# Eighteen column pairs of a SwiGLU gate/up stage as Strassen-Winograd block products, with an earlier LayerNorm sum moved between engines

## The chip, the cores and the metric

The kernel runs on one NeuronCore of a Trainium2 chip. The metric is the device time of one execution in microseconds (us), as a median over several executions. Five engines work side by side and wait for each other through semaphores: TensorE (PE in the profile; its weight loads are PEld), VectorE (DVE), ScalarE (ACT), GpSimd (POOL) and SyncE (SP, which here only issues DMAs). The program fixes the order of instructions on each of PE, DVE, ACT and POOL; an instruction that must wait holds up everything behind it on its own engine.

## The reference, cut to what matters

One layer of a hybrid decoder trunk: a modulated input projection, a convolution branch, dilated attention, a gated merge, a residual with LayerNorm (LN1), a modulated SwiGLU feed-forward network (FFN) and a second residual with LayerNorm. The change touches LN1 and the FFN:

```python
x = layer_norm(DN_ALPHA * x + (1 + g1) * y, ln1_g, ln1_b)
u = x * (1 + sc2) + sh2
h = (jax.nn.silu(u @ w_gate) * (u @ w_up)) @ w_down
x = layer_norm(DN_ALPHA * x + (1 + g2) * h, ln2_g, ln2_b)
```

There are 544 tokens (512 of a prompt, 32 of samples), `D_MODEL` is 1024 and `D_FF` is 2816, so 22 blocks of 128 columns. Everything is float32 in and out.

## The kernel before, in words

Activations lie transposed, channels on the 128 partitions and tokens on the free axis, and the tokens are cut into two halves h of 272. A float32 product is made from two fp32r parts of each operand: a high part, which ACT makes by a cast, and a low part, source minus high part, which DVE makes by a subtraction. A block of a matmul is then three matmuls: high weights by high data, high weights by low data, low weights by high data. `mm_group` (line 191) does this for a weight tile of eight 128x128 blocks along the inner dimension k: 8 x 3 matmuls of 272 columns for each half, 48 for both halves, each with its own weight load.

Weight tiles come through one stream in a fixed order: `load_more` (109) issues the DMA of a tile on SP as soon as one of four raw buffers is free, `prep_to` (119) splits a tile (ACT cast, line 131, then DVE subtraction, line 132) into one of three high and three low buffers, and `w_next` (138) hands out a tile and prepares up to three tiles ahead. Tiles of a kind other than None have places of their own, and are prepared only once a flag says that the place exists.

The output projection stage (loop at line 970) runs eight output blocks m for h = 0, then eight for h = 1. Each result is added to `z` (L983, and L987 and L989 for the samples). The class `Stats` (860) collects the LayerNorm sums on the way: at m = 3 a provisional mean by a matmul with ones (L887), by which `z` is shifted (L875), then sums `lns` of `z` (L878) and `lnq` of its squares (ACT L870, POOL L879). For h = 0 the engine of both sums is POOL; for h = 1 `lns` is on DVE. `finish` (904) ends the sums, adds over the partitions by matmuls with ones (L919, L920), and subtracts the mean (POOL L931, DVE L929). `ln1_gen` (935) then makes for each k the normalised value (DVE L946), the modulated input `u2` (ACT L948, for the samples POOL L950 and L951), its high part (ACT L952) and its low part (DVE L942), and for h = 1 turns `z` into the residual's input on POOL (L956). The generator is advanced between the blocks of the next stage.

The FFN (loop at line 1042) runs in three chunks of 8, 7 and 7 column blocks f. For each f the gate tile and the up tile are multiplied with `u2` of both halves, 96 matmuls, and `gu_evict` (1003) makes silu(gate) x up from the four PSUM tiles: sigmoid on ACT (L1008), two products on DVE (L1010, L1012), then the high part H on ACT (L1014) and the low part on DVE (L1016). After the f of a chunk, eight blocks m of the down projection over that chunk are added to `z` (`down_evict`, 1018). The first two f of the first chunk are split: the four tiles are first multiplied with half 0 alone (`first`, four PSUM tiles of the pool `pmm`), while LN1 of half 1 ends; then k by k with half 1 (`second`, lines 1061 to 1067, four PSUM tiles of other pools). The last chunk's down projection runs half by half, with the second LayerNorm's sums. Its weights are kept in places of their own (`wd0`, `wd1`), the first four prepared from the flag at line 1084 on.

`copies` (183) spreads DMA copies of the caches over the run; ACT issues them.

## Time and profile before

| | |
|---|---|
| median of 3 runs | 1046.74 us (1046.41 to 1048.29) |
| the profiled execution's own time | 1048.44 us |
| its span, first to last instruction | 1046.4 us |
| granted TensorE clock, mean | 0.990 |
| matmul instructions | 9168 |
| HBM read and written | 231.36 MB and 97.58 MB |

In the groups of instructions a line gives the source line, the engine, the operation, the tiles written and read, the shape of output and input and the count; then the busy time in us, the mean duration of one in ns, and the idle time of the engine just before, with what ended it. In the timeline a line gives the start and the duration in us; instructions of one line in a row are merged (x2), and the brackets hold the idle time before and what ended it. In the windows a line gives the stretch, its length, then for PE, PEld, DVE, ACT and POOL the busy time and count, the granted clock, the DMA share and GB/s. A matmul's duration contains its time in the pipeline; the distance from one start to the next is what it costs in a row of them. Durations of neighbouring DVE and POOL instructions overlap a little too, so there as well the distance of starts is the cost of one.

### The profile page before, as it was taken

Reading aid. Unit: us, or ns where it says so; the run is one execution under the profiler, and the core shown is the slowest. Engines: PE = TensorE matmul, PEld = TensorE weight load, DVE = VectorE, ACT = ScalarE, POOL = GpSimd, SP = SyncE. Lnnn points to the kernel's source line nnn. Section 1 sums busy time; section 2 is a strip of 40 time slices with the busy share of each in tenths; the row PEclk is TensorE's granted clock in tenths of the full one; section 3 lists DMA queues with packets and bytes.
Section 4 is the critical chain, followed back from the end, with each engine's and each line's share of the span. In section 5 each row is a group of like instructions: output and inputs, shape, how many; then the busy total and the mean of one; then the engine's idle time right before and its main releaser. Section 6 shows DMA issues by size and latency. Waiting matters only on the chain.

```text
span 1046.4 us, 21532 instructions
## 1 busy us (share of the span) xinstructions
PE 1006.8 (96%) x9168; PEld 964.8 (92%) x9168; DVE 564.4 (54%) x988; ACT 416.1 (40%) x798; POOL 153.4 (15%) x226
## 2 busy tenths in 40 slices
PE   4999999999999999999999989999999999999995
PEld 3887899999988989999999989999999999999994
DVE  3422688879886563342229767544333344344487
ACT  3312235545457666543433446422122231132333
POOL 0201010010014400101103747000000000000046
PEclk8999999999999999999999999999999999999998
DMA  9898687786785664799933710547854767754402
GB/s 379 328 387 323 248 299 257 257 330 238 279 304 187 214 258 152 293 362 391 374 123 122 246 42 21 200 163 259 287 196 167 251 231 266 252 188 172 127 15 86
DMA packets 44943, 242.64 MB, mean 232 GB/s; under 512 B 7408, under 2 KB 10736, under 8 KB 37680
## 3 DMA queue, kind: packets, MB, share of 16 engines
q1 hardware_dynamic: 34592, 126.83, 33.9%
q10 hardware_dynamic: 7632, 88.43, 23.2%
q0 software_dynamic: 2624, 26.02, 6.2%
q8 instruction: 72, 1.18, 0.4%
q14 instruction: 23, 0.19, 0.0%
HBM read 231.36 MB, written 97.58 MB: 314 GB/s over the span
## 4 chain that ended last, share of the span: by engine, by line
PE 78%; DVE 10%; ACT 5%; POOL 3%; issue 2%; DMA 2%; ACTq 0%; DVEq 0%; POOLq 0%
PE mm L196 23%; PE mm L197 22%; PE mm L199 22%; PE od L737 2%; PE Sd L702 2%; PE adaps L331 1%; DVE mrg L826 1%; DMA wr<-in_w_in 1%; PE pt L513 1%; DVE wl L132 1%; DMA cst<-in_cst 1%; PE o L529 1%; DVE z L1031 1%; DVE lns L878 1%; DVE P L498 1%
## 5 line engine op out<-in xcount | busy, mean ns | idle before, releaser
L196 PE MATMUL mm<-u,wh 128*128 128x272 f32 x1528 | 419.7, 292 | 0.0
L197 PE MATMUL mm<-u,wh 128*128 128x272 f32 x1528 | 412.5, 288 | 0.0
L199 PE MATMUL mm<-u,wl 128*128 128x272 f32 x1528 | 317.8, 288 | 0.0
L196 PEld LDWEIGHTS mm<-u,wh 128*128 128x128 f32 x1528 | 288.0, 188 | 14.2 <-issue 11.0
L197 PEld LDWEIGHTS mm<-u,wh 128*128 128x128 f32 x1528 | 287.9, 188 | 0.2
L199 PEld LDWEIGHTS mm<-u,wl 128*128 128x128 f32 x1528 | 239.7, 188 | 0.0
L132 DVE TENSOR_TENSOR wl<-wr,wh 128x1024 fp32r<-128x1024 f32 (+2 forms) x132 | 155.2, 1177 | 154.9 <-ACT wh L131 154.1
L131 ACT CAST wh<-wr 128x1024 fp32r<-128x1024 f32 (+2 forms) x132 | 130.5, 991 | 161.4 <-PE mm L197 135.7
L436 DVE SCALAR_TENSOR_TENSOR convy<-glu,vec,convy 128x512 f32<-128x512 f32 x120 | 95.6, 796 | 2.5
L197 PE MATMUL mm<-h,wh 128*128 128x272 f32 x240 | 64.8, 288 | 0.0
L196 PE MATMUL mm<-h,wh 128*128 128x272 f32 x240 | 64.5, 287 | 0.0
L1014 ACT CAST h<-sgf 128x272 fp32r<-128x272 f32 x44 | 17.0, 420 | 103.2 <-DVE sgf L1012 103.2
L896 POOL TENSOR_TENSOR lnq<-lnq,lnsq 128x272 f32<-128x272 f32 x4 | 3.1, 778 | 365.6 <-ACT lnsq L870 365.6
L1012 DVE TENSOR_TENSOR sgf<-sgf,mm 128x272 f32<-128x272 f32 x44 | 17.4, 434 | 63.3 <-PE mm L199 63.0
L1021 DVE SCALAR_TENSOR_TENSOR z<-mm,modT,z 128x272 f32<-128x272 f32 (+1 forms) x48 | 21.7, 479 | 55.5 <-PE mm L199 55.5
L199 PE MATMUL mm<-h,wl 128*128 128x272 f32 x240 | 49.6, 288 | 0.0
L634 ACT ACTIVATE qk<-mm,vec 128x272 f32<-128x272 f32 (+1 forms) x48 | 25.9, 626 | 56.6 <-PE mm L199 56.6
L196 PEld LDWEIGHTS mm<-h,wh 128*128 128x128 f32 x240 | 45.2, 188 | 0.0
L197 PEld LDWEIGHTS mm<-h,wh 128*128 128x128 f32 x240 | 45.2, 188 | 0.0
L506 ACT ACTIVATE P<-P,st 128x256 f32<-128x256 f32 x64 | 31.2, 489 | 28.2 <-DVE st L500 25.7
L197 PE MATMUL mm<-mrg,wo 128*128 128x272 f32 x128 | 37.8, 296 | 1.7 <-DVE mrg L826 1.7
L196 PE MATMUL mm<-mrg,wo 128*128 128x272 f32 x128 | 38.3, 299 | 0.0
(270 smaller groups left out, 1625.9 us busy)
## 6 DMA issues: line engine op xcount, KB each, us to landing
out_s<-in_c ACTq DMA_DIRECT2D x32, 2044.0 KB, 9.0
wr<-in_w_in SPq DMA_DIRECT2D x60, 512.0 KB, 6.9
wr<-in_w_gu SPq DMA_DIRECT2D x44, 512.0 KB, 4.8
KT<-in_kt SPq DMA_DIRECT2D x24, 792.0 KB, 7.0
VV<-in_vv SPq DMA_DIRECT2D x24, 768.0 KB, 7.5
gb<-in_w_ada POOLq DMA_DIRECT2D x8, 2048.0 KB, 16.7
...
```

Source lines behind the costliest of these rows:

```text
L131: act.copy(out=hv, in_=raw)
L132: dve.tensor_tensor(out=lv, in0=raw, in1=hv.bitcast(F32), op=ALU.subtract)
L196: pe.matmul(ps[h][:, :HC], lhsT=hi[:, k], rhs=A[h][:, 0, k], start=(k == 0), stop=False)
L197: pe.matmul(ps[h][:, :HC], lhsT=hi[:, k], rhs=A[h][:, 1, k], start=False, stop=False)
L199: pe.matmul(ps[h][:, :HC], lhsT=lo[:, k], rhs=A[h][:, 0, k], start=False, stop=(k == nk - 1))
L436: dve.scalar_tensor_tensor(out=o, in0=src, scalar=sc, in1=o, op0=ALU.mult, op1=ALU.add)
L506: act.activation(out=p[:, a:b], in_=p[:, a:b], func=AF.Exp, bias=st[:, kd, s, hh, 0:1], accum_out=st[:, kd, s, hh, 1:2])
L634: act.activation(out=o, in_=src, func=AF.Identity, bias=V("b_in", col))
L702: pe.matmul(S[32 * c:32 * c + 32, 132 * g:132 * g + 132], lhsT=q[:, col:col + 32], rhs=KT[:, j, c], start=(t == 0), stop=(j == 0 or t == 3))
L737: pe.matmul(o[32 * c:32 * c + 32, :], lhsT=lhsT, rhs=rhs, start=(j == 0), stop=(j == 9))
L1012: dve.tensor_tensor(out=sg[h], in0=sg[h], in1=pu[h][:, :HC], op=ALU.mult)
L1021: dve.scalar_tensor_tensor(out=zz[:, :n1], in0=ps[:, :n1], scalar=modT[:, 5, m, 0:1], in1=zz[:, :n1], op0=ALU.mult, op1=ALU.add)
```

## The change

For f = 3 to 20 the gate and up product of one f is taken as a product of 2x2 blocks. Rows are gate and up, columns are the token halves, the inner dimension is cut into k = 0..3 and 4..7. A11, A12 are the two k halves of the gate tile, A21, A22 those of the up tile; B11, B21 are the k halves of `u2` of half 0, B12, B22 those of half 1. Seven products of such blocks, 12 matmuls each, stand for eight:

- on the weight side POOL makes for each f S1 = A21 + A22, S2 = S1 - A11, S3 = A11 - A21, S4 = A12 - S2, each 128x512, in a ring `SS` of three buffers;
- on the data side four sums are made once: T1 = B12 - B11 (for S1), T2 = B22 - T1 (for S2), T3 = B22 - B12 (for S3), T4 = B21 - T2 (for A22). For this a tile `tf` takes B11 and B21 in one piece again (two POOL additions of 128x1088 of high and low part, issued after m = 3 of h = 1 of the output projection), and `ln1_gen` writes `u2a` of half 1 into it;
- the seven weight blocks, called units, are split one by one (ACT cast, DVE subtraction of 128x512), five units ahead of their use (`LEAD`), and the sums of f + 1 and its first five units are made during the products of f;
- `seven` adds the products in four PSUM tiles X, Zd, Y, Zc: A11 and A12 into X, S1 and S4 into Zd, S2 into Y, S3 and A22 into Zc, and builds the four results between the products, as each is due: X is gate of half 0, U2 = (first state of X) + Y, up of half 1 is U2 + Zc + Zd before their second products, up of half 0 is U2 + Zc after it, gate of half 1 is U2 + Zd after it. The last three steps (`rest`: p3, e1, e2) run during the first three products of the next f.

Blocks f = 0, 1, 2 and 21 stay as they were. In the down stages of the first two chunks the first units of the next f are made after m = 5, 6 and 7. H lies in the same two big tiles in all chunks. The flag of `wd0` is now set after f = 21. In LN1, `lns` of h = 0 goes from POOL to DVE, and L956 becomes eight POOL instructions `idle_work` during f = 3 and 4. One small scratch tile (`csg`) shares a buffer now.

```diff
--- before.py
+++ after.py
...
@@ -154,7 +156,8 @@
...
-            add_w(I["w_gu"][i], 8, ("gu", "gu", i - 3) if 3 <= i < 7 else None)
+            gu_at[i] = len(stream)
+            add_w(I["w_gu"][i], 8, ("gu", f"gu{i - 3}", 0) if 3 <= i < 5 else ("winograd",) if 6 <= i < 42 else None)
...
     def ln1_gen(h, stats):
         sd = yield from stats.finish(False, (0, 2) if h else ())
...
         for k in range(8):
...
             dve.tensor_tensor(out=zk, in0=zk, in1=sd, op=ALU.mult)
-            ak = a[k] = tmp4.tile([128, 512], F32, tag="P", name="u2a")[:, :HC]
+            ak = a[k] = tmp4.tile([128, 512], F32, tag="P", name="u2a")[:, :HC] if h == 0 else TF[0][:, 2 + k // 4, k % 4]
             act.activation(out=ak[:, :n1], in_=zk[:, :n1], func=AF.Identity, scale=G9[:, k, 0:1], bias=B9[:, k, 0:1])
             if h == 1:
...
-            if h == 1:
-                pool.tensor_scalar(out=zk, in0=zk, scalar1=agb[:, 0, k:k + 1], scalar2=agb[:, 1, k:k + 1], op0=ALU.mult, op1=ALU.add)
...
     wo = []
     for h in range(2):
-        stats = Stats(h, dve if h else pool)
+        stats = Stats(h, dve)
...
             if h == 1 and m == 3:
-                res["gu"] = [big_tile(i, [128, 4, 8, 128], F32R, f"gu{i}") for i in (0, 1)]
-                flags.add("gu")
+                TF.append(big_tile(0, [128, 4, 4, HC], F32, "tf"))
+                for i in range(2):
+                    pool.tensor_tensor(out=TF[0][:, i], in0=f32(u2[0][:, 0, 4 * i:4 * i + 4]),
+                                       in1=f32(u2[0][:, 1, 4 * i:4 * i + 4]), op=ALU.add)
...
+    UNITS = ("A11", "S1", "S2", "S3", "A12", "A22", "S4")
+    LEAD = 5
...
+    def add_up(f, n):
+        g, u = raw_of(f)
+        o = sums[f, n] = own["SS"][:, len(sums) % 3]
+        x, y, op = {
+            "S1": lambda: (u[:, 0:4], u[:, 4:8], ALU.add),
+            "S2": lambda: (sums[f, "S1"], g[:, 0:4], ALU.subtract),
+            "S3": lambda: (g[:, 0:4], u[:, 0:4], ALU.subtract),
+            "S4": lambda: (g[:, 4:8], sums[f, "S2"], ALU.subtract),
+        }[n]()
+        pool.tensor_tensor(out=o, in0=x, in1=y, op=op)
...
+    def unit_low():
+        if los:
+            f, j = los.pop(0)
+            hi, lo = place[f, j]
+            dve.tensor_tensor(out=lo, in0=src_of(f, UNITS[j]), in1=f32(hi), op=ALU.subtract)
+            if UNITS[j] == "A22":
+                assert (f, "S4") in sums
+                i = gu_at[2 * f]
+                done[i] = done[i + 1] = True
+                load_more()
+                assert pos["prep"] == i
+                pos["prep"] = i + 2
+
+    def unit_high(f, j):
...
+        else:
+            if j // 2 not in ring:
+                ring[j // 2] = (whp.tile([128, 8, 128], F32R, tag="wh", name="wh"), wlp.tile([128, 8, 128], F32R, tag="wl", name="wl"))
+            at = tuple(t[:, 4 * (j % 2):4 * (j % 2) + 4] for t in ring[j // 2])
+        place[f, j] = at
+        act.copy(out=at[0], in_=src_of(f, UNITS[j]))
+        los.append((f, j))
...
+    def product(f, j, ps, first):
+        hi, lo = place.pop((f, j))
+        B = rhs_of(UNITS[j])
+        for k in range(4):
+            pe.matmul(ps[:, :HC], lhsT=hi[:, k], rhs=B[:, 0, k], start=(first and k == 0), stop=False, skip_group_check=not first)
+            pe.matmul(ps[:, :HC], lhsT=hi[:, k], rhs=B[:, 1, k], start=False, stop=False, skip_group_check=not first)
+            pe.matmul(ps[:, :HC], lhsT=lo[:, k], rhs=B[:, 0, k], start=False, stop=(k == 3), skip_group_check=not first)
...
+    def seven(f, fi, Hs, coming, hooks):
+        X, Zd, Y, Zc = [pmm.tile([128, 512], F32, tag="mm", name="mm") for _ in range(4)]
...
+        def p1():
+            act.copy(out=s1, in_=X[:, :HC])
+
+        def p6():
+            tt(U2, s1, Y[:, :HC], ALU.add)
+
+        def p7():
+            tt(C22, U2, Zc[:, :HC], ALU.add)
+            tt(C22, C22, Zd[:, :HC], ALU.add)
+
+        def p2():
+            act.activation(out=sg0, in_=X[:, :HC], func=AF.Sigmoid)
+            tt(sg0, sg0, X[:, :HC], ALU.mult)
+
+        def p4():
+            tt(C21, U2, Zc[:, :HC], ALU.add)
+            tt(sg0, sg0, C21, ALU.mult)
+            act.copy(out=Hs[0][:, 0, fi], in_=sg0)
+
+        def p3():
+            tt(Hs[0][:, 1, fi], sg0, f32(Hs[0][:, 0, fi]), ALU.subtract)
+            tt(C12, U2, Zd[:, :HC], ALU.add)
+            act.activation(out=sg1, in_=C12, func=AF.Sigmoid)
+
+        def e1():
+            tt(sg1, sg1, C12, ALU.mult)
+            tt(sg1, sg1, C22, ALU.mult)
+            act.copy(out=Hs[1][:, 0, fi], in_=sg1)
+
+        def e2():
+            tt(Hs[1][:, 1, fi], sg1, f32(Hs[1][:, 0, fi]), ALU.subtract)
+
+        tgt = (X, Zd, Y, Zc, X, Zc, Zd)
+        after = ((), (p1,), (), (p6,), (p7,), (p2,), (p4,))
+        for j in range(7):
+            product(f, j, tgt[j], j < 4)
+            unit_low()
+            if j == 0:
+                add_up(f, "S4")
+                if f + 1 in coming:
+                    add_up(f + 1, "S1")
+            elif j in (1, 3) and f + 1 in coming:
+                add_up(f + 1, ("S2", "S3")[j // 2])
+            n = j + LEAD
+            if n < 7:
+                unit_high(f, n)
+            elif f + 1 in coming:
+                unit_high(f + 1, n - 7)
+            if rest:
+                rest.pop(0)()
+            for g in after[j]:
+                g()
+            if j in hooks:
+                hooks[j]()
+            if idle_work and j > 2:
+                idle_work.pop(0)()
+        rest.extend((p3, e1, e2))
+        pos["use"] += 2
+
...
     for j, (k0, k1) in enumerate(FF_CHUNKS):
...
-        H = [big_tile(slots[j][h], [128, 2, 8, HC], F32R, f"h{j}{h}") for h in range(2)]
-        f0 = 0
+        H = [big_tile(2 + h, [128, 2, 8, HC], F32R, f"h{j}{h}") for h in range(2)]
+        wg = [f for f in range(k0, k1) if 3 <= f < 21]
...
             gw = [w_next(1) for _ in range(4)]
             first = []
...
+            tf, f = TF[0], 3
+            TB = big_tile(1, [128, 2, 2, 4, HC], F32R, "tb")
+            T["S1"], T["S2"] = TB[:, 0], TB[:, 1]
+            t3 = one.tile([128, 4, HC], F32, tag="vT", name="t3")
+            t4 = one.tile([128, 4, HC], F32, tag="osb", name="t4")
             prep_to(pos["use"] + 1)
-            for f in range(2):
-                gu_evict({0: first[2 * f]}, {0: first[2 * f + 1]}, H, f)
-            prep_to(pos["use"] + PLOOK)
+            pool.tensor_tensor(out=t3, in0=tf[:, 3], in1=tf[:, 2], op=ALU.subtract)
+            for i in range(2):
+                gu_evict({0: first[2 * i]}, {0: first[2 * i + 1]}, H, i)
+            dve.tensor_tensor(out=tf[:, 0], in0=tf[:, 2], in1=tf[:, 0], op=ALU.subtract)
+            act.copy(out=T["S1"][:, 0], in_=tf[:, 0])
+            dve.tensor_tensor(out=tf[:, 3], in0=tf[:, 3], in1=tf[:, 0], op=ALU.subtract)
+            pool.tensor_tensor(out=t4, in0=tf[:, 1], in1=tf[:, 3], op=ALU.subtract)
+            act.copy(out=T["S2"][:, 0], in_=tf[:, 3])
+            dve.tensor_tensor(out=T["S1"][:, 1], in0=tf[:, 0], in1=f32(T["S1"][:, 0]), op=ALU.subtract)
+            dve.tensor_tensor(out=T["S2"][:, 1], in0=tf[:, 3], in1=f32(T["S2"][:, 0]), op=ALU.subtract)
             A = u2[1]
             for k in range(8):
                 for i in range(4):
@@ -1065,23 +1234,62 @@
                     pe.matmul(ps, lhsT=hi[:, k], rhs=A[:, 0, k], start=(k == 0), stop=False)
                     pe.matmul(ps, lhsT=lo[:, k], rhs=A[:, 0, k], start=False, stop=False)
                     pe.matmul(ps, lhsT=hi[:, k], rhs=A[:, 1, k], start=False, stop=(k == 7))
-            for f in range(2):
...
-        for f in range(f0, nf):
+            pg = mm_group(w_next(2), u2, 8)
+            TA = big_tile(0, [128, 2, 2, 4, HC], F32R, "ta")
+            T["S3"], T["A22"] = TA[:, 0], TA[:, 1]
+            act.copy(out=T["S3"][:, 0], in_=t3)
+            gu_evict({1: second[0]}, {1: second[1]}, H, 0)
+            dve.tensor_tensor(out=T["S3"][:, 1], in0=t3, in1=f32(T["S3"][:, 0]), op=ALU.subtract)
+            act.copy(out=T["A22"][:, 0], in_=t4)
+            own["SS"] = one.tile([128, 3, 4, 128], F32, tag="vT", name="ss")
+            for n in ("S1", "S2", "S3"):
+                add_up(f, n)
+            gu_evict({1: second[2]}, {1: second[3]}, H, 1)
+            dve.tensor_tensor(out=T["A22"][:, 1], in0=t4, in1=f32(T["A22"][:, 0]), op=ALU.subtract)
+            own["S4"] = one.tile([128, 2, 4, 128], F32R, tag="osb", name="s4")
+            pu = mm_group(w_next(1), u2, 8)
+            for n in range(4):
+                unit(f, n)
+            gu_evict(pg, pu, H, 2)
+            unit(f, 4)
+            for k in range(8):
...
+                    out=zk, in0=zk, scalar1=agb[:, 0, k:k + 1], scalar2=agb[:, 1, k:k + 1], op0=ALU.mult, op1=ALU.add))
+        for f in wg:
+            hooks = {}
+            if f == wg[-1]:
+                u = pos["use"] + 2
+                hooks = {2: lambda: prep_to(u + 1), 4: lambda: prep_to(u + 2)}
+            seven(f, f - k0, H, wg, hooks)
+            copies(0.8)
+        ring.clear()
+        if j == 2:
...
             pg = mm_group(w_next(), u2, 8)
             pu = mm_group(w_next(), u2, 8)
-            gu_evict(pg, pu, H, f)
+            gu_evict(pg, pu, H, nf - 1)
             copies(0.8)
...
+            res["wd0"] = [big_tile(i, [128, 4, 8, 128], F32R, f"wd0{i}") for i in (0, 1)]
+            flags.add("wd0")
...
+            flush()
             for m in range(8):
                 ps = mm_group(w_next(), H, nf)
...
-        if j == 1:
-            res["wd0"] = [big_tile(i, [128, 4, 8, 128], F32R, f"wd0{i}") for i in (0, 1)]
-            flags.add("wd0")
+                if m == 5:
+                    add_up(k1, "S1")
+                    add_up(k1, "S2")
+                    add_up(k1, "S3")
+                    unit(k1, 0)
+                    unit(k1, 1)
+                if m == 6:
+                    unit(k1, 2)
+                    unit(k1, 3)
+                if m == 7:
+                    unit(k1, 4)
...
```

More of the change, by code (lines that the diff above doesn't have):

```diff
@@ L205, in hybrid_step_kernel @@
     ct = const.tile([128, 8, 9], F32, name="ct")
-    csg = const.tile([128, 8, 9], F32, name="csg")
+    csg = tmp.tile([128, HC], F32, tag="ln", name="csg")[:, :72].rearrange("p (k b) -> p k b", k=8)
     cpad = const.tile([128, 8, 32], F32, name="cpad")
@@ L933, in finish, with f32 @@
             return sd
+    TF = []
+    def f32(ap):
+        return ap.bitcast(F32)
     def ln1_gen(h, stats):
@@ new lines, in unit_high, with unit @@
+    def unit_high(f, j):
+        if UNITS[j] == "S4":
+            at = (own["S4"][:, 0], own["S4"][:, 1])
+        else:
[5 more added lines that the diff above has]
+        los.append((f, j))
+    def unit(f, j):
+        unit_high(f, j)
+        unit_low()
@@ new lines, in small, with flush, tt @@
+    def small(pool_, tag):
+        return pool_.tile([128, NT if tag == "w" else 512], F32, tag=tag, name="wg")[:, :HC]
+    rest = []
+    idle_work = []
+    def flush():
+        while rest:
+            rest.pop(0)()
+    def seven(f, fi, Hs, coming, hooks):
+        X, Zd, Y, Zc = [pmm.tile([128, 512], F32, tag="mm", name="mm") for _ in range(4)]
+        s1, U2, C22, C21, C12 = small(tmp, "PT"), small(tmp4, "P"), small(tmp4, "P"), small(tmp, "PT"), small(tmp4, "P")
+        sg0, sg1 = small(tmp, "w"), small(tmp, "w")
+        def tt(o, a, b, op):
+            dve.tensor_tensor(out=o, in0=a, in1=b, op=op)
+        def p1():
[26 more added lines that the diff above has]
+            product(f, j, tgt[j], j < 4)
+            unit_low()
+            if j == 0:
[10 more added lines that the diff above has]
+            if rest:
+                rest.pop(0)()
+            for g in after[j]:
[6 more added lines that the diff above has]
+        pos["use"] += 2
```

27 lines of the change are left out of this document (23 added, 4 removed).

## The prediction

> **What bounds the kernel now.** First the busy times of the page, then the windows over the seven gate/up pairs of the second chunk, to see which engine has room in the stage that is changed.
>
> ```profile
> PE 1006.8 (96%) x9168; PEld 964.8 (92%) x9168; DVE 564.4 (54%) x988; ACT 416.1 (40%) x798; POOL 153.4 (15%) x226
> ```
> ```profile
> core 0: us, PE busy (x) PEld busy (x) DVE busy (x) ACT busy (x) POOL busy (x), PEclk, DMA share, GB/s
> 776.78:861.07 84.29, 84.29 (x674) 84.29 (x673) 32.28 (x56) 23.01 (x40) 0.00 (x0) 1.00 0.63 218
> 624.60:635.40 10.80, 10.69 (x85) 10.47 (x83) 10.49 (x27) 7.00 (x17) 5.37 (x7) 1.00 0.00 0
> 572.00:577.40 5.40, 3.66 (x27) 3.22 (x26) 5.33 (x10) 1.16 (x3) 1.28 (x1) 1.00 0.53 178
> 577.44:580.84 3.40, 3.40 (x18) 3.40 (x17) 2.41 (x4) 3.26 (x5) 1.12 (x1) 0.50 1.01 410
> ```
>
> PE has no gap in the gate/up stage: 84.29 us for 7 x 96 matmuls is 12.04 us a pair, 0.1254 us a matmul. DVE is busy 32.28 us there, 4.6 us a pair, and POOL not at all. So a matmul less is 0.1254 us less, as long as DVE and POOL can take what replaces it. The second row is the end of LN1's sums for half 1, where DVE is full (10.49 of 10.80 us). The last two are for a rival.
>
> **The change part by part.** These rows price the new work.
>
> ```profile
> L132 DVE TENSOR_TENSOR wl<-wr,wh 128x512 fp32r<-128x512 f32 x6 | 4.1, 682 | 2.9 <-ACT wh L131 2.9
> L1016 DVE TENSOR_TENSOR h<-sgf,h 128x272 fp32r<-128x272 f32 x44 | 17.6, 439 | 4.7 <-ACT h L1014 1.9
> L1012 DVE TENSOR_TENSOR sgf<-sgf,mm 128x272 f32<-128x272 f32 x44 | 17.4, 434 | 63.3 <-PE mm L199 63.0
> L896 POOL TENSOR_TENSOR lnq<-lnq,lnsq 128x272 f32<-128x272 f32 x4 | 3.1, 778 | 365.6 <-ACT lnsq L870 365.6
> L458 POOL TENSOR_TENSOR convy<-convy 128x1088 f32<-128x1088 f32 x2 | 5.1, 2552 | 2.9 <-ACT convy L457 2.9
> L956 POOL TENSOR_SCALAR z<-z,agb 128x272 f32<-128x272 f32 x8 | 4.5, 566 | 0.0
> L131 ACT CAST wh<-wr 128x512 fp32r<-128x512 f32 x6 | 3.7, 616 | 1.6 <-issue 1.6
> ```
> ```profile
> 558.32 1.60 DVE L826 TENSOR_TENSOR mrg<-mg,mrg 128x272 fp32r<-128x272 f32 x1
> 559.84 0.68 DVE L132 TENSOR_TENSOR wl<-wr,wh 128x512 fp32r<-128x512 f32 x1
> 560.44 0.90 DVE L833 SCALAR_TENSOR_TENSOR mg<-mm,vec,ga 128x272 f32<-128x272 f32 x2
> 988.38 0.80 DVE L1016 TENSOR_TENSOR h<-sgf,h 128x272 fp32r<-128x272 f32 x2
> 655.72 0.44 DVE L1010 TENSOR_TENSOR sgf<-sgf,mm 128x272 f32<-128x272 f32 x1 [0.48 <-ACT sgf L1008]
> 656.19 0.44 DVE L1012 TENSOR_TENSOR sgf<-sgf,mm 128x272 f32<-128x272 f32 x1
> 659.88 2.36 DVE L132 TENSOR_TENSOR gu<-wr,gu 128x1024 fp32r<-128x1024 f32 x2 [0.51 <-ACT gu L131]
> ```
> ```profile
> 558.21 1.40 POOL L842 TENSOR_TENSOR mg<-mg,t 128x544 f32<-128x544 f32 x1 [1.89 <-DVE mg L833]
> ```
>
> In a row, a 128x512 low part costs DVE 0.60 us (559.84 to 560.44), a 128x272 instruction 0.36 (two take 0.80 of which one is 0.44), or 0.48 where it uses the result of the one before (655.72 to 656.19). A 1024 one costs 1.14 (2.36 less 1.22). A POOL addition of 128x512 is not in the trace; between 778 ns at 272 and 2552 at 1088 it is 1.30 us.
>
> The row that decides is L826: 1.60 us for an instruction that takes 0.44, because L842 on POOL began 0.11 us earlier; it ended at 559.92, 0.30 us after L842 (559.61). Both inputs of L826 lie in SBUF. L833 and L1012, with one input in PSUM, keep their time. So DVE and POOL take turns where DVE reads two SBUF tiles. [...]
>
> *Matmuls.* 18 pairs lose 12 each: 216 x 0.1254 = 27.1 us less. A pair would take 84 x 0.1254 = 10.53 us.
>
> *DVE in a pair.* Seven low parts (4.2), eight independent 272 instructions (2.9) and three dependent ones (1.4): 8.5 us against 4.6 before. POOL: four additions, 5.2 us. ACT: seven casts and five small steps, about 6.3 us; it has room. Of DVE's 18 instructions six have an input in PSUM (p6, both of p7, p2's product, the first of p4, C12 in p3) and can run beside POOL. Now the order. The ring of three lets POOL begin S3 when the low part of S4 is done, S4 when that of S1 is, and the next pair's S1 and S2 when those of S2 and S3 are. Behind the first stand e2 and a low part, so DVE waits 1.2 us; behind the second p7 runs beside (0.84) and the next low part waits 0.55; behind the third p2 runs beside (0.36), 1.0; behind the fourth only p4's first, 0.9. That makes 3.65 us of waiting, 12.15 us in all; with gaps between engines I take 12.3. The floor, all six beside POOL, is 8.5 + 5.2 - 2.4 = 11.3; the ceiling, none beside, 13.7.
>
> Who waits for DVE: the second product of the next pair opens Zd anew, and C12, the last reader of Zd, stands in DVE's queue behind the low part of the unit before and H's. PE has 1.5 us from the end of one pair to that product, so it runs at DVE's pace and waits 12.3 - 10.53 = 1.8 us a pair. Not in every pair: the last of a chunk has no next units to make, and the first begins with five units ready (its follower waits about 0.9). With 5, 7 and 6 pairs: 12 x 1.8 + 3 x 0.9 = 24.3 us given back. L956's eight instructions of 0.57 us now take turns with DVE in f = 3 and 4: 4.5 us, half of it on the path, 2.0.
>
> *LN1's first sums.*
>
> ```profile
> PE lnps L919 <- POOL lns L878: 2.8, 1, 2.8
> PE lnps L919 <- DVE lns L878: 0.3, 1, 0.3
> PE mm L1065 <- ACT u L952: 0.2, 1, 0.2
> ```
> ```profile
> 618.64 0.44 DVE L942 TENSOR_TENSOR u<-u2a,u 128x272 fp32r<-128x272 f32 x1 [0.18 <-ACT u L952]
> 619.61 0.44 DVE L942 TENSOR_TENSOR u<-u2a,u 128x272 fp32r<-128x272 f32 x1 [0.53 <-ACT u L952]
> 624.24 0.44 DVE L942 TENSOR_TENSOR u<-u2a,u 128x272 fp32r<-128x272 f32 x1 [0.53 <-ACT u L952]
> 625.25 0.19 DVE L989 TENSOR_TENSOR z<-z,zsa 128x32 f32<-128x32 f32 x1
> 653.05 0.44 DVE L942 TENSOR_TENSOR u<-u2a,u 128x272 fp32r<-128x272 f32 x1 [0.90 <-ACT u L952]
> ```
>
> PE waits 2.8 us for POOL's `lns` of half 0. POOL loses 7 of 14 additions, DVE gains 7 x 0.48 in a stretch where it also waits for POOL's `lnq`; I expect 2.5 of the 2.8 to go (bounds 0 and 2.9).
>
> *Putting B11 and B21 together.* Two POOL additions of 128x1088, 2.55 us each. The first can begin when the low part of k = 3 is done (618.64 here, and 0.44), and the next one (619.61), with two SBUF inputs, waits for it, 2.0 us. The second follows the last low part of `u2` of half 0 (624.24) and catches the small L989 of m = 3 (625.25), 2.2 us. From there DVE is full to the end of the sums (window 624.60:635.40), and PE's next wait, L919 behind DVE's `lns`, had only 0.3 us: 4.2 us late (bounds 0 and 5.1).
>
> *Start of the loop.* After LN1's last low part (653.05 here), DVE's queue is: T3 on POOL in the way (2.4 us left), the low part of tile 4 (1.14), two evictions of `first` (3.55, as from 655.72 on here), two differences of 128x1088 (1.21 each), the low part of T1 (1.21), T4 on POOL (2.5), the low part of T2 (1.2), that of tile 5 (1.14): 15.6 us. PE needs tile 5 for the up product of f = 2, after the rest of `second` (5 us, as LN1's steps no longer wait for L956) and one gate product (6.0): about 4.3 us of waiting. Then the evictions of `second` (3.5), the low parts of T3 and T4 (2.4), four units (2.4) and four POOL additions that block 3.9: 12.2 us until L1010 reads the gate result of f = 2, whose PSUM tile X needs. PE has 5.5 us of up product left: 6.7 us. Together 11.0 (without any lock 3.6; at most 14).
>
> *End.*
>
> ```profile
> 987.39 0.29 PE L196 MATMUL mm<-h,wd 128*128 128x272 f32 x1
> 988.61 3.47 ACT L131 CAST wd<-wr 128x896 fp32r<-128x896 f32 x4
> 989.58 1.09 DVE L132 TENSOR_TENSOR wd<-wr,wd 128x896 fp32r<-128x896 f32 x1 [0.40 <-ACT wd L131]
> ```
>
> PE starts the last down projection at 987.39 with `wd` blocks split before; the third in line is split at 988.61 to 990.67, behind the last eviction. With the flag after f = 21 the first one stands at that place: PE waits until 990.67, 3.2 us.
>
> *Loads.* A raw pair is now held until its A22 is split, one product into its own pair; the next sums on it are due some 7 us later.
>
> ```profile
> wr<-in_w_gu SPq DMA_DIRECT2D x44, 512.0 KB, 4.8
> ```
>
> 4.8 us from issue to landing hides there; nothing is charged.
>
> **Sum.** -27.1 + 24.3 + 2.0 - 2.5 + 4.2 + 11.0 + 3.2 = +15.1 us. The profiled execution (1048.44 us, of which the span is 1046.4) is 0.16% above the median of 1046.74, to which I add: 1061.8 us.
>
> **Rivals.** *PE keeps its pace (faster).* If POOL's additions fall beside the six PSUM instructions or into DVE's pauses, so that DVE waits under 2.0 us a pair (10.53 - 8.5), the 24.3 and the 2.0 vanish, and the start costs 3.6 to 5: 1046.7 - 27.1 - 2.5 + 2 + 4 + 3.2 = 1026 us. For it: POOL is empty in this stage and has 10.5 us for 5.2. Against: the ring ties each addition to a DVE low part with few PSUM instructions behind it. A partial form, 11.3 to 11.7 us a pair with a start of 8, gives 1040 to 1048.
>
> *The waits cost clock too.* In the rows quoted first, PE was busy 3.66 of 5.40 us, and in the next 3.40 us it was granted 0.50 of the clock and did 18 matmuls where 27 fit, 1.1 us lost. [...] The 2.8 us wait before L919 left the clock at 1.00, which speaks against it for the loop's 1.8 us waits.
>
> **How the numbers follow.** DVE and POOL set the pace: 0.58 (of it 0.15 with the clock's loss as well), 1050 to 1074. The partial form: 0.17, 1038 to 1050. PE keeps its pace: 0.25, 1024 to 1038. A measurement of this kernel tells about 0.2% (2 us) from no change. Faster by more than that: 0.25 and a third of 0.17, 0.31; the same 0.05; slower 0.64. The range that leaves out the fastest forms and the worst start is 1030 to 1074; the likeliest case's own is 1050 to 1074.
>
> **What would show it.** In the profile after: DVE busy above 85% with POOL near 42% in the gate/up windows, low parts (now one line in `unit_low`) with a mean of 0.9 us or more rather than 0.68, a PE wait for DVE before the second product of most pairs, windows of a 7-pair stage near 83.6 us where 73.7 would be PE's pace; one wait of PE at the up product of f = 2 and one before f = 3; the 2.8 us wait for POOL gone and one of some 4 us at the second L919; 3 us before the last down projection. The forecast is wrong if the 7-pair stage takes 75 us or less: then the lock did not bind the loop.

## The result and the profile after

| | before | after |
|---|---|---|
| median | 1047.08 us (1046.41 to 1048.29, 4 runs) | 1055.93 us (1055.41 to 1058.17, 4 runs) |
| ratio of the times | | 1.0088, 95% interval 1.0076 to 1.0101 |
| profiled execution, its span | 1048.44, 1046.4 | 1055.41, 1053.5 |
| granted TensorE clock, mean | 0.990 | 0.984 |
| matmul instructions | 9168 | 8952 |

The kernel became 0.9% slower: 8.9 us between the medians, 7.1 between the two profiled spans. (The median before is 1047.08 us here with one run more than in the table further up.) The page's busy times of the changed kernel:

```profile
PE 988.6 (94%) x8952; PEld 943.6 (90%) x8952; DVE 696.1 (66%) x1181; ACT 461.9 (44%) x910; POOL 260.1 (25%) x295
```

To see where the 7.1 us arose, I cut both spans at instructions that both kernels have: the first matmul that adds LN1's sums over the partitions for half 0 and for half 1 (L919 before, L922 after), and the first matmul of each down projection. The start times come from the timelines. The forecast's terms are split by the pairs of a chunk: 1.51 us less for each of 5, 7 and 6 pairs, 1.8 us of waiting in 3, 5 and 4 of them and 0.9 in one of each chunk.

| stretch | before | after | difference | foreseen |
|---|---|---|---|---|
| start to LN1's end, half 0 | 606.16 | 603.09 | -3.07 | -2.5 |
| to LN1's end, half 1 | 29.38 | 33.20 | +3.82 | +4.2 |
| to the first down projection (start, 5 pairs) | 93.23 | 101.52 | +8.29 | +11.8 |
| to the second (down, 7 pairs) | 132.30 | 129.18 | -3.12 | -0.6 |
| to the third (down, 6 pairs) | 126.32 | 124.91 | -1.41 | -0.9 and a wait |
| to the end | 59.05 | 61.61 | +2.56 | with that wait 3.2 |

The seven pairs of the second chunk, and eight stretches of 3.41 us to which I come back, in the windows of the changed kernel:

```profile
core 0: us, PE busy (x) PEld busy (x) DVE busy (x) ACT busy (x) POOL busy (x), PEclk, DMA share, GB/s
785.82:867.00 81.18, 75.66 (x591) 74.36 (x590) 74.82 (x123) 38.61 (x80) 30.95 (x22) 1.00 0.61 218
...
634.79:638.20 3.41, 1.91 (x10) 1.51 (x11) 2.84 (x6) 2.05 (x4) 2.29 (x4) 1.00 0.00 0
638.20:641.61 3.41, 3.41 (x29) 3.41 (x28) 3.41 (x4) 0.52 (x1) 3.41 (x4) 1.00 0.55 159
600.66:604.07 3.41, 0.98 (x5) 0.87 (x5) 3.01 (x6) 0.68 (x2) 1.08 (x1) 1.00 0.62 181
604.07:607.48 3.41, 3.41 (x16) 3.40 (x15) 1.55 (x2) 2.24 (x4) 2.90 (x5) 0.50 0.38 136
...
665.51:668.92 3.41, 2.22 (x10) 2.22 (x11) 2.43 (x6) 2.27 (x4) 0.00 (x0) 0.50 0.25 85
...
679.16:682.57 3.41, 3.36 (x15) 3.36 (x16) 3.27 (x7) 2.56 (x6) 2.06 (x2) 0.50 0.00 0
989.78:993.19 3.41, 0.75 (x4) 0.46 (x4) 2.88 (x6) 2.94 (x5) 0.00 (x0) 1.00 0.27 96
993.19:996.60 3.41, 3.41 (x16) 3.41 (x17) 1.79 (x2) 1.40 (x3) 0.00 (x0) 0.50 0.78 252
```

84.29 us became 81.18, not the 73.7 that seven products a pair would take at PE's pace. DVE is now busy for 92% of the stage and PE has gaps. What PE waits for, in the changed kernel:

```profile
PE mm L1111 <- DVE wg L1131: 12.7, 10, 1.4
...
PE lnps L922 <- DVE lns L881: 4.9, 2, 3.1
PE mm L1111 <- DVE sgf L1018: 4.2, 1, 4.2
PE mm L202 <- DVE wl L134: 3.0, 1, 3.0
...
PE mm L199 <- ACT wd L133: 2.0, 1, 2.0
...
PE mm L202 <- DVE wd L134: 0.6, 1, 0.6
```

In order of time these are: LN1's sums of both halves (L922), tile 5 at the start of the loop (L202), the first product of f = 3 (L1018 must read the gate of f = 2 out of the PSUM tile first), ten waits of up to 1.4 us in the pairs, and the late blocks of `wd0`. The place of the ten is seen in PE's timeline, in the third pair of the second chunk:

```profile
814.80 0.29 PE L1113 MATMUL mm<-u,wl 128*128 128x272 f32 x1
816.53 0.39 PE L1111 MATMUL mm<-ta,wh 128*128 128x272 f32 x1 [1.44 <-DVE wg L1131]
```

It is the sixth product, A22 (its data is `ta`), which opens the PSUM tile Zc again and needs p7's reading of it (L1131). Zd, at which the prediction had the wait, is not waited for.

The turns of DVE and POOL stand in the groups. First the low parts and the small steps on DVE, then POOL's sums:

```profile
L1083 DVE TENSOR_TENSOR wl<-wr,wh 128x512 fp32r<-128x512 f32 x54 | 49.4, 920 | 4.6 <-ACT wh L1100 4.3
L1083 DVE TENSOR_TENSOR wl<-ss,wh 128x512 fp32r<-128x512 f32 x54 | 48.8, 910 | 0.0
L1131 DVE TENSOR_TENSOR wg<-wg,mm 128x272 f32<-128x272 f32 x108 | 46.4, 429 | 8.0 <-PE mm L1113 5.9 <-ACT wg L1144 1.1
L1131 DVE TENSOR_TENSOR wg<-wg 128x272 f32<-128x272 f32 x54 | 37.2, 689 | 2.9 <-ACT wg L1155 1.7
L1131 DVE TENSOR_TENSOR h<-wg,h 128x272 fp32r<-128x272 f32 x36 | 17.8, 495 | 2.9 <-ACT h L1160 1.5 <-ACT h L1150 1.5
...
L1073 POOL TENSOR_TENSOR ss<-wr 128x512 f32<-128x512 f32 x36 | 53.1, 1476 | 149.8 <-DMA wr<-in_w_gu 82.3 <-DVE s L1083 41.1 <-DVE wl L1083 8.8
```

The same operation on the same shape takes 429 ns where one input is PSUM (`mm`) and 689 ns where both are SBUF. One case in the timeline of both engines, with the same pair of instructions ahead of it, when POOL was idle:

```profile
836.10 0.91 DVE L1131 TENSOR_TENSOR wg<-wg 128x272 f32<-128x272 f32 x2
...
845.84 1.69 POOL L1073 TENSOR_TENSOR ss<-wr 128x512 f32<-128x512 f32 x1 [3.81 <-DMA wr<-in_w_gu]
846.29 2.98 DVE L1131 TENSOR_TENSOR wg<-wg 128x272 f32<-128x272 f32 x2
847.61 1.37 POOL L1073 TENSOR_TENSOR ss<-ss,wr 128x512 f32<-128x512 f32 x1
```

Two steps of 0.91 us take 2.98 while POOL makes S1 and S2. The whole trace says the same: of the 54 steps on two SBUF inputs (`wg<-wg`), the 40 with no POOL instruction beside them took 426 to 445 ns, the 14 with one took 1065 to 1537. Of the 108 steps with a PSUM input, 50 had POOL beside them and took 431 ns on average, the other 58 took 428. POOL's S1 could begin only when the weights had landed (the bracket); the prediction had charged nothing for loads.

The two POOL additions that put B11 and B21 together (L1003, 616.10 and 623.64, 2.5 us each) stop DVE in the same way. A low part that takes 0.44 us otherwise and a step on 32 columns that takes 0.19 were held until the addition was over:

```profile
616.48 2.44 DVE L950 TENSOR_TENSOR u<-u2a,u 128x272 fp32r<-128x272 f32 x1 [0.53 <-ACT u L960]
```
```profile
624.13 2.08 DVE L995 TENSOR_TENSOR z<-z,zsa 128x32 f32<-128x32 f32 x1
```

### The profile page after: what moved, and what is told of

Same layout as the page of the kernel before. It is cut to its first block, busy times and chain, and to the rows that moved or that the text cites. A ratio compares the mean times of both kernels' runs of the same rounds, so it can differ in the third digit from the quotient of the medians.

```text
span 1053.5 us, 21611 instructions
## 1 busy us (share of the span) xinstructions
PE 988.6 (94%) x8952; PEld 943.6 (90%) x8952; DVE 696.1 (66%) x1181; ACT 461.9 (44%) x910; POOL 260.1 (25%) x295
## 4 chain that ended last, share of the span: by engine, by line
PE 62%; DVE 23%; ACT 7%; issue 3%; DMA 2%; POOL 2%; ACTq 0%; DVEq 0%; SPq 0%; POOLq 0%
PE mm L199 15%; PE mm L200 14%; PE mm L202 14%; DVE wl L1083 5%; DVE wg L1131 5%; PE mm L1111 2%; PE mm L1112 2%; PE mm L1113 2%; PE od L740 2%; PE Sd L705 2%; PE adaps L334 1%; DMA wr<-in_w_in 1%; DVE mrg L829 1%; ACT wh L1100 1%; PE pt L516 1%
## 5 line engine op out<-in xcount | busy, mean ns | idle before, releaser
L199 PE MATMUL mm<-u,wh 128*128 128x272 f32 x984 | 274.7, 296 | 1.1 <-DVE zsa L993 0.7
L200 PE MATMUL mm<-u,wh 128*128 128x272 f32 x984 | 267.3, 289 | 0.0
L202 PE MATMUL mm<-u,wl 128*128 128x272 f32 x984 | 206.4, 290 | 3.0 <-DVE wl L134 3.0
L199 PEld LDWEIGHTS mm<-u,wh 128*128 128x128 f32 x984 | 186.3, 189 | 15.7 <-issue 11.8
L200 PEld LDWEIGHTS mm<-u,wh 128*128 128x128 f32 x984 | 186.6, 190 | 0.2
L202 PEld LDWEIGHTS mm<-u,wl 128*128 128x128 f32 x984 | 155.5, 189 | 3.2 <-DVE wl L134 3.2
L1073 POOL TENSOR_TENSOR ss<-wr 128x512 f32<-128x512 f32 x36 | 53.1, 1476 | 149.8 <-DMA wr<-in_w_gu 82.3
L1111 PE MATMUL mm<-ta,wh 128*128 128x272 f32 x144 | 42.9, 298 | 12.9 <-DVE wg L1131 12.7
L1083 DVE TENSOR_TENSOR wl<-wr,wh 128x512 fp32r<-128x512 f32 x54 | 49.4, 920 | 4.6 <-ACT wh L1100 4.3
L1131 DVE TENSOR_TENSOR wg<-wg,mm 128x272 f32<-128x272 f32 x108 | 46.4, 429 | 8.0 <-PE mm L1113 5.9
L202 PE MATMUL mm<-h,wl 128*128 128x272 f32 x240 | 49.6, 288 | 0.0
L1083 DVE TENSOR_TENSOR wl<-ss,wh 128x512 fp32r<-128x512 f32 x54 | 48.8, 910 | 0.0
L1111 PE MATMUL mm<-u,wh 128*128 128x272 f32 x144 | 42.3, 293 | 4.2 <-DVE sgf L1018 4.2
L199 PEld LDWEIGHTS mm<-h,wh 128*128 128x128 f32 x240 | 45.2, 188 | 0.0
```

Of the source, the lines that this page charges most:

```text
L199: pe.matmul(ps[h][:, :HC], lhsT=hi[:, k], rhs=A[h][:, 0, k], start=(k == 0), stop=False)
L200: pe.matmul(ps[h][:, :HC], lhsT=hi[:, k], rhs=A[h][:, 1, k], start=False, stop=False)
L202: pe.matmul(ps[h][:, :HC], lhsT=lo[:, k], rhs=A[h][:, 0, k], start=False, stop=(k == nk - 1))
L1073: pool.tensor_tensor(out=o, in0=x, in1=y, op=op)
L1083: dve.tensor_tensor(out=lo, in0=src_of(f, UNITS[j]), in1=f32(hi), op=ALU.subtract)
L1111: pe.matmul(ps[:, :HC], lhsT=hi[:, k], rhs=B[:, 0, k], start=(first and k == 0), stop=False, skip_group_check=not first)
```

## The experiments

Theory: DVE and POOL take turns where DVE reads two SBUF tiles (1065 to 1537 ns instead of 426 to 445 in the changed kernel); a POOL sum therefore costs DVE its whole length, and these turns set the pace of the pairs. Rivals: DVE's own work, or a chain from the weights' landing to the product, sets it. For the start of the loop the theory was that each of PE's waits has one step of DVE behind it and can be taken away by itself; the rival, that DVE is behind as a whole. This theory fell in the runs. Ratios are to the kernel before, which was timed again beside each group of runs (medians 1046.7 to 1048.2 us); so compare runs by their ratios where the times differ by a few us.

**Without POOL's sums.**

```diff
-        pool.tensor_tensor(out=o, in0=x, in1=y, op=op)
+        if f == 3:
+            pool.tensor_tensor(out=o, in0=x, in1=y, op=op)
```

> Leaves out POOL's sums S1 to S4 for every tile but f = 3 (the units read what f = 3 left in the three buffers), so the output of those tiles is another; every DVE, ACT and PE instruction and every load stays. Theory (DVE and POOL take turns, and these turns set the pace): DVE has 8.5 us of work a pair against PE's 10.53, the pairs run at PE's pace, about 10.6 us instead of 12.0 to 12.5, the 7-pair stage at about 75 us instead of 81.2, PE's 12.7 us of waits before the products go to under 3, low parts average 0.68 us instead of 0.92; time about 1043 us, 13 less than the changed kernel. Rival (the length of DVE's own queue, or the late arrival of the weights, sets the pace): 7-pair stage above 79 us, time 1053 or more.

Measured: 1039.48 us, ratio 0.9928 (0.9915 to 0.9940). The window of the seven pairs, and the groups:

```profile
783.01:857.12 74.11, 74.11 (x590) 74.11 (x589) 60.70 (x123) 39.85 (x80) 0.00 (x0) 1.00 0.67 243
```
```profile
L1132 DVE TENSOR_TENSOR wg<-wg,mm 128x272 f32<-128x272 f32 x108 | 47.1, 436 | 25.4 <-PE mm L1114 17.5 <-ACT wg L1145 7.2
L1084 DVE TENSOR_TENSOR wl<-wr,wh 128x512 fp32r<-128x512 f32 x54 | 38.0, 707 | 4.9 <-ACT wh L1101 4.6
L1084 DVE TENSOR_TENSOR wl<-ss,wh 128x512 fp32r<-128x512 f32 x54 | 37.7, 703 | 0.0
L1132 DVE TENSOR_TENSOR wg<-wg 128x272 f32<-128x272 f32 x54 | 23.8, 441 | 2.9 <-ACT wg L1156 1.7
L1132 DVE TENSOR_TENSOR h<-wg,h 128x272 fp32r<-128x272 f32 x36 | 15.7, 436 | 2.9 <-ACT h L1161 1.5 <-ACT h L1151 1.5
```

PE has no gap. Compared with the changed kernel's groups, low parts fall from 920 to 707 ns and the small SBUF steps from 689 to 441; the steps with PSUM stay (429, 436). Over the seven pairs DVE is busy 60.70 us instead of 74.82, so 30.95 us of POOL's work had cost it 14.1 us: a sum costs DVE time only where it meets a step on two SBUF tiles, not its whole length each time. This stage also measures the saving in matmuls by itself: 84.29 - 74.11 = 10.18 us for seven pairs, 1.45 a pair, 26.2 us for 18.

**Sums made, but read by nobody.**

```diff
+        if f > 3 and n[0] == "S":
+            return {"S1": u[:, 0:4], "S2": g[:, 0:4], "S3": g[:, 0:4], "S4": g[:, 4:8]}[n]
```

> POOL still makes every sum, but for f > 3 the units S1 to S4 are split from raw blocks of the weights, so nobody waits for a sum and no sum waits for a unit (the output of these tiles is another). Theory (turns): the 5.2 us of POOL a pair still stand in DVE's way, 7-pair stage 80 to 82.5 us, low parts still at 0.9 us on average, time 1053 to 1057. Rival (the chain weights landed, sum on POOL, high part, low part, product is what is late): the pairs go to PE's pace, 7-pair stage about 75 us, time about 1043.

Measured: 1063.64 us, ratio 1.0161 (1.0147 to 1.0175), slower still than the change itself. The window of its seven pairs, then groups:

```profile
788.92:872.45 83.53, 76.93 (x591) 74.55 (x589) 77.37 (x123) 38.28 (x80) 29.96 (x20) 1.00 0.61 214
```
```profile
L1133 DVE TENSOR_TENSOR wg<-wg 128x272 f32<-128x272 f32 x54 | 40.0, 741 | 2.9 <-ACT wg L1157 1.7
L1133 DVE TENSOR_TENSOR h<-wg,h 128x272 fp32r<-128x272 f32 x36 | 24.4, 677 | 2.9 <-ACT h L1152 1.5 <-ACT h L1162 1.5
```

This and the run before have the same DVE, ACT and PE instructions; POOL's sums, which nobody waits for, cost 24 us, and DVE's busy time over the seven pairs rises from 60.70 to 77.37 us. From 780 to 1000 us no wait of another engine, nor of the queue that issues the loads, ends with POOL. That rules the chain through the sums out as the cause, and shows the turns. I had expected the time of the changed kernel; freed from waiting for DVE, the sums fall upon the small steps more often (h<-wg,h 677 ns, 495 in the changed kernel).

**The sums on DVE.**

```diff
-        pool.tensor_tensor(out=o, in0=x, in1=y, op=op)
+        (pool if f == 3 and n != "S4" else dve).tensor_tensor(out=o, in0=x, in1=y, op=op)
...
-                if f + 1 in coming:
-                    add_up(f + 1, "S1")
-            elif j in (1, 3) and f + 1 in coming:
-                add_up(f + 1, ("S2", "S3")[j // 2])
+            elif j in (2, 3, 4) and f + 1 in coming:
+                add_up(f + 1, ("S1", "S2", "S3")[j - 2])
```

> All sums of f > 3, and S4 of f = 3, move from POOL to DVE (S1, S2, S3 behind products 2, 3 and 4 instead of 0, 1 and 3). Theory (turns): DVE has 8.5 + 4 x 0.60 = 10.9 us a pair and waits for nobody, so pairs take 10.9 to 11.2 us, the 7-pair stage 76 to 78.5 us; POOL empty in it; time 1045 to 1049. Rival (DVE is the bound by its own work, POOL's help counts more than the turns cost): pairs of 12.3 us or more, no gain, 1056 to 1061.

Measured: 1042.78 us, ratio 0.9960 (0.9948 to 0.9973): faster than the kernel before. Window, then the group of the sums:

```profile
781.61:857.34 75.73, 75.58 (x591) 74.37 (x590) 73.03 (x148) 39.74 (x80) 0.00 (x0) 1.00 0.67 237
```
```profile
L1073 DVE TENSOR_TENSOR ss<-wr 128x512 f32<-128x512 f32 x34 | 23.2, 683 | 0.0
```

10.82 us a pair: DVE is full (96%), and yet 5.5 us faster over the seven pairs than with the work shared. A sum costs 0.60 us on DVE (the prediction's price of a 128x512 step in a row) and 1.35 to 1.48 on POOL in the changed kernel, its own waits for DVE included, 2.2 to 2.5 times as long; and a 128x272 step on two SBUF tiles that met a POOL instruction there took DVE 1.07 to 1.54 us instead of 0.43 to 0.45. It is these turns that decide.

**The order at the start.**

```diff
+            sg2 = gu_half(pg)
             for n in range(4):
                 unit(f, n)
-            gu_evict(pg, pu, H, 2)
+            gu_rest(sg2, pu, H, 2)
```

The low parts of T1 and T2 also move behind the first `w_next(2)` (tile 5); `gu_half` and `gu_rest` are the two parts of `gu_evict`, cut behind L1018.

> At the start of the loop only: the low parts of T1 and T2 stand behind the low part of weight tile 5 instead of ahead of it, and the sigmoid product of the gate of f = 2 stands ahead of the four units instead of behind them. Theory (DVE's order at the start is what PE waits for): the 3.2 us wait for the low part of tile 5 shrinks to 1 or less, the 4.2 us wait behind the sigmoid product to 1 or less, and the half-clock windows at 665 to 672 and 679 us go: 5 to 8 us less, 1048 to 1051. Rival (PE then waits for the units instead, as DVE's work there is the same in sum): the waits move to the first product, gain under 2 us, 1054 to 1056.

Measured: 1057.45 us, ratio 1.0090 (1.0076 to 1.0104): nothing gained, a miss. PE's longest wait of the loop in this kernel:

```profile
PE mm L1118 <- DVE sgf L1021: 5.8, 1, 5.8
```

The wait for tile 5 is 0.8 us now instead of 3.0, and what was saved is waited for behind it: 5.8 us before the first product instead of 4.2, and 5.7 us in the pairs of the first chunk where the changed kernel waits 3.3. The rival holds.

**The flag of `wd0` ahead of f = 21 again** (the two lines of the flag stand before the last gate product).

> Only the place of the wd0 flag: before f = 21 again instead of behind it. Theory: the splits of the first down blocks are made in time, PE's 2.0 us wait for their high part and the 0.6 us for the low part go, and with them the half-clock window at 993 us (1.2 us): 3 to 4.7 us less, 1051 to 1053. Rival (the splits then stand in the way of the last pair's units or evictions on ACT and DVE): PE waits there instead, gain under 1 us.

Measured: 1051.60 us, ratio 1.0034 (1.0021 to 1.0047; the changed kernel has 1.0088), as expected. PE waits for no `wd` block, and the last two stretches take 122.57 and 59.11 us instead of 124.91 and 61.61: 4.8 us.

**LN1's sums of half 0 back on POOL** (`Stats(h, dve if h else pool)`).

> Undoes one part: LN1's first sums of half 0 on POOL again. By the prediction's term (-2.5 us for the move) the time would rise by 2 to 3 us, to 1058 to 1059. By the trace of the changed kernel (PE waited 3.2 us for DVE's last sum where it had waited 2.8 us for POOL's) the move gained nothing: within 1 us of the changed kernel, 1055 to 1057, and the half-clock window behind that wait goes if the wait comes out under 3 us.

Measured: 1057.55 us, ratio 1.0090 (1.0077 to 1.0103), the time of the changed kernel. PE's wait here:

```profile
PE lnps L922 <- POOL lns L881: 2.7, 1, 2.7
```

2.7 us for POOL, or 3.1 for DVE: the sums are late on either engine. The move gains nothing. The mean granted clock of the profiled execution is 0.984, as in the changed kernel; that the half-clock window behind this wait went, though the wait is under 3 us now, isn't shown.

**Without putting B11 and B21 together** (T1 by two subtractions on DVE, T4 by two steps on POOL, straight from the high and low halves).

> B11 and B21 aren't put together ahead of the loop: T1 is made on DVE by two subtractions from the high and low halves, T4 by two POOL steps, and the two POOL additions of 128x1088 in the out stage go. Theory: the 2.6 us lost at LN1's sums of half 1 go, DVE has 1.2 us more and POOL 2.5 us more at the start of the loop, of which up to 1.2 us can be late there: 1.4 to 2.6 us less, 1053 to 1055. Rival (the additions lie beside other work and cost nothing): no gain, or 1 to 3 us more through the longer start.

Measured: 1056.92 us, ratio 1.0084 (1.0070 to 1.0098): no gain, a miss. LN1's end of half 1 comes 3.0 us sooner (stretch of 30.24 us instead of 33.20), and PE gives most of it back at tile 5, where it waited 3.0 us, and a little before the first product, 4.6 instead of 4.2:

```profile
PE mm L202 <- DVE wl L134: 5.2, 1, 5.2
```

**Four edits together, and two of them.**

> The sums on DVE, the new order at the start, the wd0 flag ahead of f = 21 and T1 and T4 without the additions, all four together. If the four places are independent, as the chain of waits has it, their gains add up: 8 + 6 + 4 + 2 = 20 us less than the changed kernel, about 1036 us, faster than the kernel before by 1.0%. Rival (what is gained at one place is lost at the next, since DVE is the late engine at each): 1045 or more, at best equal to the kernel before.

Measured: 1038.33 us, ratio 0.9911 (0.9898 to 0.9923). Of the four, the sums and the flag:

> The sums on DVE and the wd0 flag ahead of f = 21, without the new order at the start and without dropping the additions that put B11 and B21 together. By the chunk ends of the runs so far (from the second half of the first two tiles' products to the last product of the first chunk: 81.5 us in the changed kernel, 82.5 with the new order, 77.4 with the sums on DVE, 81.5 with all four) the two start edits gain nothing, because DVE is late from LN1's last low part to the end of the first chunk: 1037 to 1039, the same as all four together. Rival (each edit has its own gain): 1042 or more.

Measured: 1039.43 us, ratio 0.9927 (0.9913 to 0.9941): the same within the intervals. From LN1's end of half 0 to the first down projection the two need 130.82 and 130.61 us. So the start edits add nothing here either. What stands in DVE's way at the start is seen in DVE's and in POOL's timeline of the second kernel:

```profile
660.81 1.28 DVE L1225 TENSOR_TENSOR tb<-tf,tb 128x1088 fp32r<-128x1088 f32 x1
662.07 3.54 DVE L1226 TENSOR_TENSOR tb<-tf,tb 128x1088 fp32r<-128x1088 f32 x1
```
```profile
660.97 3.48 POOL L1223 TENSOR_TENSOR t<-tf 128x1088 f32<-128x1088 f32 x1 [7.67 <-DVE tf L1222]
```

T4 on POOL and the low parts of T1 and T2 on DVE shut each other out: T4 lies beside L1225 first and takes 3.48 us, where T3, of the same shape, takes 2.54 in this kernel (L1217); then L1226 lies beside T4 and takes 3.54, where L1225 takes 1.28.

**f = 3 as an ordinary pair**, alone and with four edits.

```diff
-("winograd",) if 6 <= i < 42
+("winograd",) if 8 <= i < 42
...
-        wg = [f for f in range(k0, k1) if 3 <= f < 21]
+        wg = [f for f in range(k0, k1) if 4 <= f < 21]
```

> The changed kernel, but f = 3 is an ordinary pair of eight block products and the seven-product form begins at f = 4. PE gets 12 matmuls more (1.5 us), DVE gets about 4 to 6 us less work while PE does them. Theory (DVE is behind at the start, and the start's waits are its arrears): the 4.2 us wait before the first product goes, the 3 us wait at tile 5 stays, first chunk 3 to 5 us shorter, time 1051 to 1053. Rival (the first waits are for one thing each, a fixed chain of DVE steps): the waits stay and 1.5 us is added, 1057.

Measured: 1056.16 us, ratio 1.0081 (1.0066 to 1.0096); the wait for the sigmoid product of f = 2 is 1.7 us instead of 4.2, but the 3 to 5 us don't show in the time. The stretch to the first down projection, 99.10 us, is 2.4 shorter in the profiled execution. The ratios (1.0081 and 1.0088, each within the other's interval) leave open whether anything is gained.

> The sums on DVE, the wd0 flag ahead of f = 21, T1 and T4 without the additions, the low parts of T1 and T2 behind tile 5's, and f = 3 as an ordinary pair. With the arrears worked off in f = 3's pair the edits of the start can show: against the kernel with all four edits, -8.4 us of wait before the first product, -1.2 of half clock behind it, +1.5 of matmuls: about 1031. If DVE is still behind at f = 4, 1035 or more.

Measured: 1040.83 us, ratio 0.9935 (0.9922 to 0.9949), a miss: not better than the same edits with seven products at f = 3. One wait holds the arrears:

```profile
PE mm L199 <- DVE sgf L1015: 10.2, 1, 10.2
```

DVE is as late as before: from LN1's end of half 1 to the first down projection this kernel needs 104.15 us, the one with four edits 101.52. The theory of single waits falls with it.

**Nothing for POOL at the start.** On top of the sums on DVE and the flag: T3, T4, the first S1 to S3 and the two additions of B11 and B21 on DVE, the eight steps on `z` on ACT.

```diff
-            pool.tensor_tensor(out=t4, in0=tf[:, 1], in1=tf[:, 3], op=ALU.subtract)
+            dve.tensor_tensor(out=t4, in0=tf[:, 1], in1=tf[:, 3], op=ALU.subtract)
...
-                idle_work.append(lambda k=k, zk=zk: pool.tensor_scalar(
-                    out=zk, in0=zk, scalar1=agb[:, 0, k:k + 1], scalar2=agb[:, 1, k:k + 1], op0=ALU.mult, op1=ALU.add))
+                idle_work.append(lambda k=k, zk=zk: act.activation(
+                    out=zk, in_=zk, func=AF.Identity, scale=agb[:, 0, k:k + 1], bias=agb[:, 1, k:k + 1]))
```

> The kernel with the sums on DVE and the wd0 flag ahead of f = 21, and of the rest that POOL got at the start of the loop: T3, T4, the first S1 to S3 and the two additions of B11 and B21 on DVE, and the eight late steps on z on ACT. POOL's trace in that kernel has these steps in DVE's way for: T3 2.0 us, T4 2.3, S1 to S3 about 2.5, the steps on z about 1.8, the additions 3.9. On DVE they cost 1.2, 1.2, 1.8, 0 and 2.4. Theory (turns: a POOL step costs DVE its whole length, twice what DVE needs itself): DVE is 4 to 6 us less late at the end of the first chunk, 1032 to 1035 (against 1037 to 1039 for the kernel without these edits). Rival (POOL's steps at the start lie beside other work, DVE gets longer by 6.6 us of its own): 1040 or more.

Measured: 1034.46 us, ratio 0.9881 (0.9865 to 0.9898), the fastest of all: 1.2% faster than the kernel before. To the first down projection 127.42 us instead of 130.61. PE still waits 2.0 us at tile 5, and before the first product:

```profile
PE mm L1111 <- DVE sgf L1018: 3.9, 1, 3.9
```

Which of the moved steps pays for how much of this, no run separates.

## Why the prediction was right, and where it was off

The direction, the cause and the range held: 1055.93 us lies in the likeliest case's own range of 1050 to 1074. 1061.8 was 5.9 us too high, and the sum of +15.1 stands against +7.1 in the spans.

- **Matmuls**, -27.1: measured -26.2 (1.45 us a pair).
- **Waits in the loop**, +24.3 and 2.0 for L956: the term that was mis-sized. Without POOL's sums PE has no gap in the pairs, and the second chunk gains 129.18 - 122.12 = 7.1 us, the first 101.52 - 97.82 = 3.7, the third 124.91 - 119.80 = 5.1. Together 16. A pair that waits lost what was forecast: the sixth products of the second chunk start at 816.53, 828.50, 841.01 and 853.29 us, 12.0 to 12.5 apart where 12.3 was forecast, against 10.6 a pair without the sums, so 1.7 us where 1.8 was forecast. But only ten pairs wait, not twelve and three in part, and nothing shows for L956 beside them. PE's wait lies four products later than the forecast put it, at the sixth product. So PE runs further ahead before DVE's lag reaches it: the first two pairs of seven hardly wait (0.1 us in the second), the last doesn't.
- **DVE's pace**: from 816.53 to 853.29 us DVE is busy 35.39 us, 11.8 a pair; without POOL's sums it is busy 26.52 us between the same products (811.75 to 843.51), 8.8 a pair (forecast 8.5). So the turns cost 3.0 us in a pair that waits (forecast 3.65), and 0.5 is idle, behind PE's products and ACT's casts (forecast 0.15); the errors cancel in part. Over all 18 pairs the turns cost less: over the 54 small SBUF steps 54 x (689 - 441), over the low parts of the two groups 54 x (920 - 707) and 54 x 0.207, and 2.1 for H: 38 us, 2.1 us a pair.
- **The reading behind it.** L833 and L1012, by which the prediction had steps with a PSUM input keep their time beside POOL, didn't show it: no POOL instruction ran beside any of them in the kernel before (L842 waits for L833). The assumption was right all the same, by the 431 and 428 ns above.
- **LN1's first sums**, -2.5: wrong. The wait changed its engine, not its length (2.8 for POOL before, 3.1 for DVE after; 2.7 with the part undone). The -3.07 us of that stretch lie ahead of the sums: the first LayerNorm matmul of the whole run already comes at 300.7 us instead of 302.6, in code that isn't changed, and the kernel before then ran 3.40 us at half the clock (577.44:580.84 in the prediction), which the changed one didn't (1.00 from 20.39 to 604.07 us). That the two numbers agree is chance.
- **Putting B11 and B21 together**, +4.2: measured +3.82 in that stretch, and 3.9 by the kernels with four edits and with two (29.30 against 33.22). Right in size and cause, as the two DVE steps that were held lost 2.0 and 1.9 us (by its own rows the second was 2.0, not 2.2). It didn't come as one wait of some 4 us: PE waits 1.8 us before the second L922 (0.3 before), and 0.7 further ahead for L993; the rest lies at the half-clock window at 604.07. The run without POOL's sums needs 33.23 us too, with 1.9 us of waiting before the second L922 and 1.9 for L993, 3.5 us more than the kernel before; so DVE sets this stretch. Taking the additions out gave no time, since the start is late by then in any case.
- **Start of the loop**, +11.0: the first product comes at 679.21 us, where the kernel before starts f = 3 at 668.58 (f = 2 at 656.21, and 96 matmuls), so 10.6 us later; 0.7 of that was there already at LN1's end of half 1, which leaves +9.9. The waits are shorter than forecast (3.0 and 4.2 us against 4.3, by its own steps 15.6 - 11.0 = 4.6, and 6.7); the two half-clock windows behind tile 5 (10 and 17 matmuls in 665.51:668.92 and 668.92:672.34, where 27 fit in each) make up for much of it. So the size is right in part by luck. Sums kept apart mislead here: the edits to single waits (the order at the start, the additions, f = 3 as a pair) moved the waits and left the time from LN1's end to the first down projection within 132.3 and 136.2 us (134.7 in the changed kernel). Only less work in DVE's way shortens it: 130.6 with the sums on DVE, 127.4 with nothing on POOL, against 122.6 before.
- **End**, +3.2: measured 4.8 with the flag put back; 2.6 us of waiting, and about 1.4 for the half-clock window at 993.19 (16 matmuls where 27 fit); the last 0.8 no run separates.
- **The clock's rival** came true in part: in LN1 and the FFN five half-clock windows, behind the waits at LN1, at tile 5 (two), before the first product and at the end, about 1.4 us for a full one, as 16 matmuls stand where 27 fit. The one at the first product isn't in any term above. With it the parts add up: -26.2 + 16 - 3.1 + 3.8 + 9.9 + 4.8 + 1.4 = 6.6 of the 7.1 us.
- **What would show it**: DVE at 92% and low parts at 0.92 us were as foreseen, POOL 38% (forecast 42%). The wait before the second product, the 83.6 us for seven pairs and the single wait of some 4 us at the second L919 were not. By the lock its last sentence means the turns of DVE and POOL, and they bound the loop: 81.18 us for seven pairs with POOL's sums, 74.11 without. A start without them, for which the prediction has 3.6 us, no run shows: with nothing for POOL there PE still waited 2.0 us at tile 5 and 3.9 before the first product.
